# Three edits to a transformer layer on one core: the sample's attention in tiles of 128 rows, the selection masks inside the first gate projections, and another order of loads at the start of the second feed-forward product

## The chip, the cores and the metric

The kernel runs on one core of a Trainium2 chip. TensorE (PE) multiplies matrices, VectorE (DVE), ScalarE (ACT) and GpSimd (POOL) do the elementwise work, and SyncE (SP) issues most of the transfers between HBM and the core's memory. The metric is the device time of one execution in microseconds, less being better. Before is given as the median of three runs.

## What is computed

One layer is applied to a prompt of 1024 rows and to a sample of 64 rows that has 128 rows of cached keys and values. Both have 1024 channels. The reference, cut to what matters here:

```python
qa, ka, va, qi, ki, wi, qb, kb, vb, ga, gb = split(rmsnorm(x) @ w_in)     # 8 heads of 64 in each mixer
# mixer a: every query keeps the 256 visible keys with the best index score (sample: 48 of 192)
isc = sum_h wi[t, h] * relu(qi[t, h] . ki[s]);  keep = top_k(isc)
oa = softmax(qa . ka / 8 over keep) @ va
# mixer b: own chunk of 64 and the 8 chunks before it, with a bias by clipped distance
ob = softmax(qb . kb / 8 + bias) @ vb
x = x + (sigmoid(ga) * (oa @ w_o_a) + sigmoid(gb) * (ob @ w_o_b)) @ w_out
x = x + square(relu(rmsnorm(x) @ w_up)) @ w_down
```

The sample's queries see 192 keys in both mixers: the 128 cached ones and their own 64. The layer also returns the keys and values that it made.

## The kernel before

Every float32 operand is split into a high part (`hi`, an ACT copy into the matmul's reduced format) and a low part (`lo = raw - hi`, on DVE or POOL). Then three matmuls, hi by hi, hi by lo and lo by hi, make one product (`three`, lines 154 to 156). `two` (lines 162 and 163) does the same with a stationary operand that already holds both parts. `split` (line 143) makes a pair, with the low part on POOL unless `lo_on_vector` is set: line 146 is DVE's form and line 148 POOL's.

The program is written in an order of its own, and a planner then fixes the order of each engine and each queue. It goes by its own costs: an instruction goes out when the planner believes its operands to be ready, and among ready ones the earlier in the program goes first. `tc.issue_after(x)` keeps instructions behind `x` on the engine that `x` runs on. On the chip every engine and queue then works strictly in the planned order.

The stages, with their place in the profiled span:

- 0 to 155 us: norms, index keys and index scores. `stage_scores(i)` makes the scores of row block i (block 8 is the sample) in four PSUM banks called `s`. Into the last two blocks the first steps of `project_heads` are mixed (`between`). A step is the product of one row block with one 512-column weight: 24 matmuls, or 16 for the sample. It takes a bank called `acc` (two of them) or `wide` (four of them, on the space of `s`). The list `turn` says which: the first `FIRST` steps take `acc`, then one of every three does.
- 155 to 440 us: the other steps of `project_heads`, in the order vb, kb, qb, ka, va, qa. The weights come through two buffers `wraw` into eleven pairs `whi` and `wlo`. Beside this, `choose` finds for each row the score of its 256th best key, by 31 rounds of bisection on DVE and ACT, and then writes the masks of row blocks 2 to 7 (lines 571 to 584). `mask_s` is that of the sample.
- 440 to 490 us: the first four of 16 gate projections (`gate`), with their weights in the same `whi` and `wlo`.
- 490 to 800 us: attention, eight heads of mixer b and then eight of mixer a. The work on a head is in five groups: four pairs of row blocks, and the sample's 64 queries. `probs` makes scores (matmuls into `s`), adds bias or mask, and forms the softmax. `weigh` transposes the probabilities by PE, splits them, and multiplies by the values `vhl` into `po`. Eight more gate projections are laid between (`next_mark`). Their weights are in the pool `ring`. `ring` and attention's pool `at` are opened after the pools `tk` (the masks' temporaries), `pj`, `works` (the scores) and `fw` are closed, and take over their space.
- 800 to 1393 us: the other gates, the output projections, and the first feed-forward product.
- 1393 to 1738 us: the second feed-forward product, in four rounds of seven products P1, P2, P5, P6, P3, P7 and P4 (Strassen's scheme in Winograd's form). A product is 4 steps of 12 matmuls. The operands of the very first, `first_ops`, are made beforehand. All others are loaded from HBM (`left_source`, `right_source`) and split into slots of the pools `fx`, `fy` and `fz`. `few_operands` loads the sample's rows, and `few_rows` multiplies them. `take` adds the results up, and the last ones go out to `y_p`.

Of the kernel before, what the change touches and what calls it, by code (L numbers as in the profile page):

```python
# [18 lines left out]
P = 128  # L19
# [13 lines left out]
RING = 5  # L33
FIRST = 3
WARM = 18
# [9 lines left out]
def kernel(  # L45
# [97 lines left out]
    def split(raw, hi, lo, lo_on_vector=False):  # L143
        copy(hi, raw)
        if lo_on_vector:
            nc.vector.tensor_sub(lo, raw, hi)  # L146
        else:
            nc.gpsimd.tensor_sub(lo, raw, hi)  # L148
# [275 lines left out]
    def values_to_dram(t, rows, dst, r0):  # L424
        both = pj.tile([P, TP], F32R, tag="pair", name="pair", bufs=3).rearrange("p (h z d) -> p h z d", h=H, z=2)
        split(t[:rows].rearrange("p (h d) -> p h d", d=HD), both[:rows, :, 0], both[:rows, :, 1])
        nc.sync.dma_start(dst[r0:r0 + rows], both.bitcast(F32)[:rows])
# [54 lines left out]
    stage_scores(NT - 1, {3: heads, 7: heads})  # L482
    stage_scores(NT, {7: heads})
    close_pool("ix")

    masks = open_pool("masks")
    mask = {i: masks.tile([P, P * (i + 1)], BF16, name=f"mask{i}") for i in range(2, NT)}
    mask_s = masks.tile([TS, 192], BF16, name="mask_s")
    diag = masks.tile([P, 256], BF16, name="diag")
    nc.gpsimd.memset(diag, 0.0)  # L490
# [28 lines left out]
    def choose(vector, scalar):  # L519
# [50 lines left out]
        nc.vector.tensor_mul(thr, bits.bitcast(F32), sgn)  # L570
        for j, (i, w) in enumerate(zip(blocks, ws)):
            n = w.shape[1]
            over, same = (tk.tile([P, TP], BF16, tag="seen", name="seen", bufs=2) for _ in range(2))
            nth = tk.tile([P, TP], F32, tag="nth", name="nth", bufs=1)
            nc.vector.tensor_scalar(w, w, col(sgn, j), None, op0=ALU.mult)
            nc.vector.tensor_scalar(over[:, :n], w, col(thr, j), 0.0, op0=ALU.is_gt, op1=ALU.add, accum_out=col(cnt, j))
# [6 lines left out]
            nc.vector.tensor_add(over[:, :n], over[:, :n], same[:, :n])  # L583
            nc.gpsimd.tensor_scalar(mask[i], over[:, :n], -1.0, BIG, op0=ALU.add, op1=ALU.mult)

    def gate(m, ws, after=None):
# [9 lines left out]
    def load_head(mix, h, pool):  # L596
# [3 lines left out]
        for z in range(2):  # L600
# [6 lines left out]
                          v[:9 * P, h].rearrange("(t p) z d -> p t z d", p=P))  # L607
        nc.sync.dma_start(vhl[:TS, 9], v[9 * P:, h].rearrange("p z d -> p (z d)"))
        if mix == "b":
# [12 lines left out]
    with tc.issue_after(state["last"].ins):  # L622
        for _ in range(TOPK_S // 8):
            m8 = tk.tile([TS, 8], F32, tag="m8", name="m8", bufs=2)
            nc.vector.max(out=m8, in_=work_s)
            nc.vector.match_replace(out=work_s, in_to_replace=m8, in_values=work_s, imm_value=TAKEN)
        nc.vector.tensor_scalar(mask_s, work_s, 0.5 * (HIDDEN + TAKEN), -BIG, op0=ALU.is_gt, op1=ALU.mult)
        choose([2, 3, 4], [5, 6, 7])
    todo = [(mix, h) for mix in "ba" for h in range(H)]
    first_head = load_head(*todo[0], kv)  # L630
    for g in range(0, EARLY, 4):
        ws = []
        for k in range(KB):
# [4 lines left out]
            split(raw, hi, lo, lo_on_vector=True)  # L638
            ws.append((hi, lo))
        for q in range(4):  # L640
            gate(g + q, [(h[:, q * P:(q + 1) * P], l[:, q * P:(q + 1) * P]) for h, l in ws])
    for nm in ("tk", "pj", "works", "fw"):
        close_pool(nm)
# [15 lines left out]
    def attention(mix, h, t):  # L659
# [29 lines left out]
        def weigh(po, units):  # L689
            n = len(units)  # L690
            done = 0
            while done < n:
# [19 lines left out]
                for oo, (srcs, vt, krows, width, qo), idx in batch:  # L712
                    dst = po[:, qo:qo + width]
                    nc.tensor.matmul(dst, vhl[:krows, vt, :], ph[:krows, oo:oo + width], start=(idx == 0), stop=False)  # L714
                    nc.tensor.matmul(dst, vhl[:krows, vt, :], pl[:krows, oo:oo + width], start=False, stop=(idx == n - 1))  # L715

        def store(po, n, c0):
            half = at.tile([HD, 256], F32, tag="half", name="half", bufs=2)
            o = at.tile([HD, 256], F32, tag="o", name="o", bufs=3)
            copy(half[:, :n], po[HD:P, :n])  # L720
            nc.vector.tensor_add(o[:, :n], po[:HD, :n], half[:, :n])
            nc.sync.dma_start(o_dram[mix][cols, c0:c0 + n], o[:, :n])

        def soften(g):
            if g == 4:
                return [probs(TS, TP, TP, 192, bias[:, 384:576] if mix == "b" else mask_s)], None
            ms, first = [], []
# [13 lines left out]
        def mix_values(g, ms, first):  # L741
            po = bank("po", 256)
            if g == 4:
                weigh(po, [([(ms[0], 0, TS)], 8, P, TS, 0), ([(ms[0], P, TS)], 9, TS, TS, 0)])
                store(po, TS, TP)
                return
# [385 lines left out]
    dc = open_pool("dc", "right", reuse_waits="tile")  # L1132
    dp = open_pool("dp", reuse_waits="tile")
    fx = open_pool("fx", reuse_waits="tile")
    yp = open_pool("yp", reuse_waits="tile")
    slot = iter([place for place in ((fx, 8), (fy, 9), (fz, 6)) for _ in range(place[1])] * 20)

# [60 lines left out]
    QUAD = NPAIR // 4  # L1198
    q = {nm: [yp.tile([P, 512], F32, name=f"q_{nm}_{t}") for t in range(4)] for nm in ("P1", "P2", "P5", "P6", "P3", "P7", "P4")}
    y_few = yp.tile([TS, D], F32, name="y_few")  # L1200
    part = {"P2": (0, 0), "P3": (0, 512), "P4": (512, 0), "x": (512, 512)}
# [8 lines left out]
    def take(g, nm, t, ps):  # L1210
# [5 lines left out]
        if nm == "P7" and last:  # L1216
# [3 lines left out]
            return  # L1220
        if nm == "P4" and last:
            nc.vector.tensor_add(mine["P6"], ps, mine["P6"])
            nc.sync.dma_start(out_place(y_p, "P4", t), mine["P6"])
            return
        nc.vector.tensor_add(mine[nm], ps, mine[nm])
# [10 lines left out]
        elif nm == "P3":  # L1236
            nc.sync.dma_start(out_place(y_p, "P3", t), mine["P3"])

    for g in range(QUAD):
        few = few_operands(g)  # L1240
        for nm in ("P1", "P2", "P5", "P6", "P3", "P7", "P4"):
            at_end = nm == "P4" and g == QUAD - 1
            sums_here = [bank("x") for _ in range(4)]
            first = g == 0 and nm == "P1"
            if nm in ("P1", "P3"):
                few_sum = bank("few")
            ops = {}

            def few_rows(k):
                for z in range(2):  # L1250
# [4 lines left out]
            for k in range(4):  # L1255
# [3 lines left out]
                else:  # L1259
                    h = down_operand(left_source(nm, p), True)  # L1260
                    w = down_operand(right_source(nm, p), k < 3)
                ops[k] = h, w
                if at_end:
                    continue
                for t in range(4):
                    tok = slice(t * P, (t + 1) * P)
                    three(sums_here[t], [((h[0][:, tok], h[1][:, tok]), w)], k == 0, k == 3)
                if nm in KIND and not first:
                    few_rows(k)
            if first:  # L1270
                for k in range(4):
                    few_rows(k)
            if g == 0 and nm in part:
                for t in range(4):
                    nc.sync.dma_start(q[nm][t], out_place(x1_dram, nm, t))
                if nm == "P2":
                    nc.sync.dma_start(y_few, x1_dram[TP:])
            for t in range(4):
                if at_end:
                    tok = slice(t * P, (t + 1) * P)  # L1280
                    three(sums_here[t], [((ops[k][0][0][:, tok], ops[k][0][1][:, tok]), ops[k][1]) for k in range(4)])
                take(g, nm, t, sums_here[t])
            if nm in ("P2", "P7"):
# [8 lines left out]
            if nm == "P7" and g == QUAD - 1:  # L1292
                nc.sync.dma_start(y_s, y_few)
    for nm in ("dc", "fy", "fz", "yp", "fx", "dp"):
        close_pool(nm)
# [36 lines left out]
```

## Time and profile before

| | |
|---|---|
| median of three runs | 1738.48 us (1738.3 to 1742.39) |
| profiled execution, its own time | 1739.78 us |
| span of the profiled execution | 1738.0 us |
| mean granted TensorE clock | 0.997 |
| busy in the span: PE, DVE, ACT, POOL | 1709.3, 1199.3, 956.4, 481.4 us |
| bytes moved | 294.97 MB, 170 GB/s on the mean |

The span runs from the first to the last instruction of the profiled execution, and its own time is 1.8 us above its span. An engine's busy time counts its instructions and not the issue of transfers. The ends of matmuls are modelled, and neighbouring ones overlap in the records. So the pace of TensorE is read from start to start, and a stall from the idle time that the trace lists before an instruction.

### The profile page before, as it was taken

How to read it: one execution, taken by the hardware profiler on the slowest of the kernel's cores; microseconds unless marked ns; L12 is line 12 of the kernel's file. 1: busy time of each engine (PE TensorE's matmuls, PEld its weight loads, DVE VectorE, ACT ScalarE, POOL GpSimd, SP SyncE). 2: the span in 40 equal slices, each digit the busy share in tenths (PEclk: the TensorE clock that was granted, in tenths of full speed). 3: DMA queues.
4: the chain of work that ended last, by engine and by line, in shares of the span. 5: the costliest groups of instructions: out<-in, count | busy, mean ns of one | idle time of the engine just before them, and what ended most of it. 6: DMA issues, size and time to landing. Idle time of an engine off the chain costs nothing.

```text
span 1738.0 us, 30914 instructions
## 1 busy us (share of the span) xinstructions
PE 1709.3 (98%) x10540; PEld 1551.3 (89%) x10540; DVE 1199.3 (69%) x2765; ACT 956.4 (55%) x1994; POOL 481.4 (28%) x549
## 2 busy tenths in 40 slices
PE   8999999999999999999999999999999999999999
PEld 6877888877999999999999999999999978888887
DVE  6776799994447777774354345865587658868787
ACT  5785889722357777776443346644454447343430
POOL 2252432545424333332344354000000011111122
PEclk9999999999999999999999999999999999999999
DMA  5022475444667876664544559555566589565643
GB/s 175 8 81 104 149 201 151 152 161 161 180 162 191 198 176 153 159 146 134 170 137 136 185 163 284 168 184 183 186 209 204 165 300 316 183 199 149 199 124 103
DMA packets 277197, 294.97 MB, mean 170 GB/s; under 512 B 39792, under 2 KB 201584, under 8 KB 277040
## 3 DMA queue, kind: packets, MB, share of 16 engines
q1 hardware_dynamic: 248064, 257.61, 51.0%
q10 hardware_dynamic: 28976, 35.40, 5.8%
q8 instruction: 83, 1.36, 0.3%
q14 instruction: 74, 0.61, 0.1%
HBM read 199.85 MB, written 93.08 MB: 169 GB/s over the span
## 4 chain that ended last, share of the span: by engine, by line
PE 85%; DVE 6%; DMA 3%; issue 3%; ACT 2%; POOL 1%; SPq 0%; ACTq 0%; DVEq 0%; POOLq 0%
PE acc L154 9%; PE acc L156 9%; PE acc L155 9%; PE x L156 5%; PE x L155 5%; PE x L154 5%; PE pt L699 4%; PE wide L154 3%; PE wide L155 3%; PE wide L156 3%; PE s L162 3%; PE po L715 2%; PE s L163 2%; PE po L714 2%; PE pg L156 2%
## 5 line engine op out<-in xcount | busy, mean ns | idle before, releaser
L155 PE MATMUL x<-lo,hi 128*128 128x512 f32 x432 | 168.8, 391 | 2.3 <-POOL lo L148 1.7
L156 PE MATMUL x<-hi,lo 128*128 128x512 f32 x432 | 166.8, 391 | 0.0
L154 PE MATMUL x<-hi 128*128 128x512 f32 x432 | 164.2, 392 | 0.0
L148 POOL TENSOR_TENSOR lo<-wr,hi 128x512 fp32r<-128x512 f32 x15 | 35.1, 2343 | 455.6 <-ACT hi L123 455.6
L148 POOL TENSOR_TENSOR lo<-raw,hi 128x512 fp32r<-128x512 f32 x88 | 117.9, 1350 | 153.7 <-ACT hi L123 145.8
L123 ACT ACTIVATE hi<-raw 128x512 fp32r<-128x512 f32 x104 | 64.3, 627 | 90.4 <-PE acc L155 21.6
L711 DVE TENSOR_TENSOR pl<-pt,ph 128x512 fp32r<-128x512 f32 (+4 forms) x184 | 96.6, 545 | 19.5 <-ACT ph L123 18.9
L536 ACT ACTIVATE nth<-work,cand 128x768 bf16<-128x768 f32 (+2 forms) x93 | 96.6, 1039 | 18.3 <-DVE cand L553 14.1
L146 DVE TENSOR_TENSOR lo<-hr,hi 128x512 fp32r<-128x512 f32 x108 | 81.6, 756 | 28.9 <-ACT hi L123 28.7
L155 PEld LDWEIGHTS x<-lo,hi 128*128 128x128 f32 x432 | 81.1, 188 | 21.2 <-POOL lo L148 2.1
L123 ACT ACTIVATE ph<-pt 128x512 fp32r<-128x512 f32 (+4 forms) x184 | 81.6, 483 | 32.4 <-PE pt L699 25.6
L156 PEld LDWEIGHTS x<-hi,lo 128*128 128x128 f32 x432 | 81.1, 188 | 17.9
L154 PEld LDWEIGHTS x<-hi 128*128 128x128 f32 x432 | 81.1, 188 | 17.6
L154 PE MATMUL acc<-xnT,hi 128*128 128x384 f32 (+1 forms) x288 | 95.5, 331 | 0.0
L156 PE MATMUL acc<-xnT,lo 128*128 128x384 f32 (+1 forms) x288 | 94.3, 327 | 0.0
L155 PE MATMUL acc<-xnT,hi 128*128 128x384 f32 (+1 forms) x288 | 94.3, 327 | 0.0
L686 POOL TENSOR_SCALAR mw<-mw,sm 128x640 f32<-128x640 f32 (+1 forms) x64 | 56.7, 886 | 131.8 <-DVE sm L685 131.7
L154 PE MATMUL wide<-whi,xnT 128*128 128x512 f32 x224 | 89.4, 404 | 1.7 <-DVE work_s L366 1.7
L156 PE MATMUL wide<-whi,xnT 128*128 128x512 f32 x224 | 90.1, 402 | 0.0
L155 PE MATMUL wide<-wlo,xnT 128*128 128x512 f32 x224 | 89.9, 401 | 0.0
L714 PE MATMUL po<-ph,vhl 128*128 128x256 f32 (+2 forms) x336 | 86.0, 274 | 0.4 <-ACT ph L123 0.4
L715 PE MATMUL po<-pl,vhl 128*128 128x256 f32 (+2 forms) x336 | 85.9, 285 | 0.6 <-DVE pl L711 0.6
(671 smaller groups left out, 5963.2 us busy)
## 6 DMA issues: line engine op xcount, KB each, us to landing
hr<-h SPq DMA_DIRECT2D x108, 256.0 KB, 3.6
wr<-in_w_down_dram SPq DMA_DIRECT2D x76, 256.0 KB, 4.0
wraw<-in_w_in_dram SPq DMA_DIRECT2D x56, 256.0 KB, 2.8
h<-h ACTq DMA_DIRECT2D x32, 272.0 KB, 2.1
raw<-in_w_out_dram SPq DMA_DIRECT2D x32, 256.0 KB, 3.0
raw<-in_w_up_dram SPq DMA_DIRECT2D x32, 256.0 KB, 3.5
out_dram<-t SPq DMA_DIRECT2D x24, 256.0 KB, 2.4
g_dram<-gate SPq DMA_DIRECT2D x32, 192.0 KB, 3.2
```

Source lines behind the costliest of these rows:

```text
L123: return nc.scalar.activation(out, in_, AF.Copy)
L146: nc.vector.tensor_sub(lo, raw, hi)
L148: nc.gpsimd.tensor_sub(lo, raw, hi)
L154: nc.tensor.matmul(out, sh, mh, start=(opens and i == 0), stop=False, skip_group_check=resumes)
L155: nc.tensor.matmul(out, sh, ml, start=False, stop=False, skip_group_check=resumes)
L156: last = nc.tensor.matmul(out, sl, mh, start=False, stop=(closes and i == n - 1), skip_group_check=resumes)
L536: nc.scalar.activation(sign[:, :w.shape[1]], w, AF.Sign, bias=against, scale=-1.0, accum_out=col(cnt, j))
L686: nc.gpsimd.tensor_scalar(m[:rows, :n], m[:rows, :n], sm[:rows, 6:7], 1.0, op0=ALU.mult, op1=ALU.mult)
L699: nc.tensor.transpose(ps[:krows, oo:oo + qrows], m[:qrows, kc:kc + krows], ident[:qrows, :qrows])
L711: nc.vector.tensor_sub(pl[:kr, a:b], ps[:kr, a:b], ph[:kr, a:b])
L714: nc.tensor.matmul(dst, vhl[:krows, vt, :], ph[:krows, oo:oo + width], start=(idx == 0), stop=False)
L715: nc.tensor.matmul(dst, vhl[:krows, vt, :], pl[:krows, oo:oo + width], start=False, stop=(idx == n - 1))
```

## The change

- Scores: `FIRST` goes from 3 to 5, and the sample's `stage_scores` gets a projection step after its fourth head too. So four steps of `project_heads` stand ahead of the opening of `wide`, not three, and the first six take `acc`.
- Masks: `choose` ends with the threshold, and the scores get their sign back by an ACT copy with a scale (before: a DVE multiplication in the loop of masks). The loop's body becomes `mask_out`, which is called after the first gates and kept behind the last `lo` of their weights. `values_to_dram` makes the low part of mixer a's values on DVE, not on POOL.
- Sample's attention: `probs` runs on 128 query rows, the prompt's last 64 and the sample's 64. The sample's mask lies in the lower half of a tile `mask_below` (one transfer), and the bias is read 64 columns on. `weigh_sample` transposes two 128 by 128 tiles that overlap by 64 keys, and multiplies by full tiles of values, the second with zeros in its upper half.
- Second feed-forward product: the operands of P2 in round 0, the rows of the residual that it is added to, and the sample's residual are loaded ahead of the sample's rows. The sample's share of P1 is done inside P2. All low parts of round 0 are made on DVE. The slots go round in the order `fx`, `fz`, `fy`, and P2's sums get a pool of their own.
- The end: the last of the four result tiles is made and sent in two halves of 256 columns, the second by ACT's queue.

```diff
-FIRST = 3
+FIRST = 5
...
     def values_to_dram(t, rows, dst, r0):
-        split(t[:rows].rearrange("p (h d) -> p h d", d=HD), both[:rows, :, 0], both[:rows, :, 1])
+        split(t[:rows].rearrange("p (h d) -> p h d", d=HD), both[:rows, :, 0], both[:rows, :, 1],
+              lo_on_vector=dst is v_dram["a"])
...
-    stage_scores(NT, {7: heads})
+    stage_scores(NT, {3: heads, 7: heads})
...
-        for j, (i, w) in enumerate(zip(blocks, ws)):
+        for j, w in enumerate(ws):
+            nc.scalar.activation(w, w, AF.Copy, scale=col(sgn, j))
+
+        def mask_out(j):
+            i, w = blocks[j], ws[j]
...
-            nc.vector.tensor_scalar(w, w, col(sgn, j), None, op0=ALU.mult)
...
+        return mask_out
...
-        nc.sync.dma_start(vhl[:TS, 9], v[9 * P:, h].rearrange("p z d -> p (z d)"))
+        nc.gpsimd.memset(vhl[:TS, 9], 0.0)
+        nc.sync.dma_start(vhl[TS:, 9], v[9 * P:, h].rearrange("p z d -> p (z d)"))
...
-        choose([2, 3, 4], [5, 6, 7])
+        mask_out = choose([2, 3, 4], [5, 6, 7])
+    nc.sync.dma_start(mask_below[TS:], mask_s)
...
+        lows = last["lo"]
         for q in range(4):
             gate(g + q, [(h[:, q * P:(q + 1) * P], l[:, q * P:(q + 1) * P]) for h, l in ws])
+
+        with tc.issue_after(lows.ins):
+            for j in range(6):
+                mask_out(j)
...
+        def weigh_sample(po, m):
+
+            ps = ptile()
+            for j in range(2):
+                nc.tensor.transpose(ps[:, j * P:(j + 1) * P], m[:, j * TS:j * TS + P], ident)
+            v = ps[:, :2 * P].rearrange("p (j q) -> p j q", j=2)[:, :, TS:]
+            ph, pl = (at.tile([P, 512], F32R, tag=nm, name=nm, bufs=4) for nm in ("ph", "pl"))
+            halves = [t[:, :P].rearrange("p (j q) -> p j q", j=2) for t in (ph, pl)]
+            copy(halves[0], v)
+            nc.vector.tensor_sub(halves[1], v, halves[0])
+            for j in range(2):
+                nc.tensor.matmul(po[:, :TS], vhl[:, 8 + j, :], ph[:, j * TS:(j + 1) * TS], start=(j == 0), stop=False)
+                nc.tensor.matmul(po[:, :TS], vhl[:, 8 + j, :], pl[:, j * TS:(j + 1) * TS], start=False, stop=(j == 1))
...
-                return [probs(TS, TP, TP, 192, bias[:, 384:576] if mix == "b" else mask_s)], None
+                return [probs(P, TP - TS, TP, 192, bias[:, 448:640] if mix == "b" else mask_below)], None
...
-                weigh(po, [([(ms[0], 0, TS)], 8, P, TS, 0), ([(ms[0], P, TS)], 9, TS, TS, 0)])
+                weigh_sample(po, ms[0])
...
+    yr = open_pool("yr", reuse_waits="tile")
...
-    slot = iter([place for place in ((fx, 8), (fy, 9), (fz, 6)) for _ in range(place[1])] * 20)
+    slot = iter([place for place in ((fx, 8), (fz, 6), (fy, 9)) for _ in range(place[1])] * 20)
...
+    loaded = [(left_source("P2", k), right_source("P2", k)) for k in range(4)]
+    residual("P2")
+    nc.sync.dma_start(y_few, x1_dram[TP:])
+    late_rows = []
     for g in range(QUAD):
         few = few_operands(g)
...
-                    h = down_operand(left_source(nm, p), True)
-                    w = down_operand(right_source(nm, p), k < 3)
+                    src = loaded[k] if second else (left_source(nm, p), right_source(nm, p))
+                    h = down_operand(src[0], True)
+                    w = down_operand(src[1], k < 3 or g == 0)
...
+                if second and k == 0:
+                    for rows_of in late_rows:
+                        rows_of()
+                if first:
+                    late_rows.append(lambda k=k, rows=few_rows: rows(k))
+                elif nm in KIND:
                     few_rows(k)
-            if first:
-                for k in range(4):
-                    few_rows(k)
...
+                tok = slice(t * P, (t + 1) * P)
+                for z, queue in enumerate((nc.sync, nc.scalar)):
+                    c = slice(256 * z, 256 * (z + 1))
+                    if t == 3 or z == 0:
+                        wide = c if t == 3 else slice(0, 512)
+                        ps = bank("x") if t == 3 and z else sums_here[t]
+                        three(ps[:, wide], [((ops[k][0][0][:, tok], ops[k][0][1][:, tok]),
+                                                       [w[:, wide] for w in ops[k][1]]) for k in range(4)])
+                        nc.vector.tensor_add(q["P6"][t][:, wide], ps[:, wide], q["P6"][t][:, wide])
+                        queue.dma_start(out_place(y_p, "P4", t)[:, wide], q["P6"][t][:, wide])
```

## Rows read from the trace of the kernel before

**Rows 1.** The page's busy time of each engine.

```profile
PE 1709.3 (98%) x10540; PEld 1551.3 (89%) x10540; DVE 1199.3 (69%) x2765; ACT 956.4 (55%) x1994; POOL 481.4 (28%) x549
```

**Rows 2.** Stretches: length, busy PE, PEld, DVE, ACT, POOL, then clock, DMA, GB/s.

```profile
150.00:155.00 5.00, 2.66 (x18) 1.55 (x16) 3.42 (x9) 2.83 (x8) 0.14 (x1) 1.00 0.00 2
155.00:160.00 5.00, 4.86 (x14) 3.89 (x15) 5.00 (x17) 0.00 (x0) 0.69 (x4) 0.66 0.24 62
380.00:400.00 20.00, 14.46 (x58) 10.67 (x57) 17.97 (x13) 9.45 (x17) 14.55 (x10) 0.96 0.76 279
400.00:420.00 20.00, 20.00 (x84) 16.09 (x83) 7.69 (x24) 5.41 (x11) 10.54 (x11) 0.95 0.56 185
460.00:480.00 20.00, 20.00 (x125) 19.68 (x124) 0.69 (x2) 5.57 (x11) 6.33 (x5) 1.00 0.77 216
1400.00:1420.00 20.00, 20.00 (x89) 16.39 (x88) 9.17 (x14) 9.18 (x16) 1.28 (x1) 1.00 0.97 320
```

**Rows 3.** PE's waits: who was waited for, us in total, times, longest.

```profile
PE acc L154 <- ACT whi L123: 4.4, 2, 3.2
PE acc L155 <- POOL wlo L148: 1.1, 1, 1.1
...
PE x L155 <- POOL lo L148: 1.7, 1, 1.7
PE x L155 <- DVE lo L146: 0.6, 1, 0.6
```

**Rows 4.** DVE's timeline, masks and gates: start, length, instruction, idle before.

```profile
357.22 0.60 DVE L576 TENSOR_SCALAR_CACHE_REDUCE seen<-work,thr 128x384 bf16<-128x384 f32 x1
...
396.09 0.67 DVE L583 TENSOR_TENSOR seen<-seen 128x1024 bf16<-128x1024 bf16 x1
...
447.40 0.68 DVE L146 TENSOR_TENSOR wlo<-wraw,whi 128x512 fp32r<-128x512 f32 x1
```

**Rows 5.** PE's timeline: attention's first matmul, then one head's sample group.

```profile
490.52 0.22 PE L162 MATMUL s<-kh,qT 128*128 128x128 f32 x1
...
529.93 0.28 PE L714 MATMUL po<-ph,vhl 128*128 128x256 f32 x1
530.14 0.33 PE L699 MATMUL pt<-ident,m 64*128 64x64 f32 x2
530.40 0.39 PE L162 MATMUL s<-kh,qT 128*128 128x256 f32 x1
...
533.35 0.19 PE L715 MATMUL po<-pl,vhl 128*128 128x64 f32 x1
533.47 0.29 PE L714 MATMUL po<-ph,vhl 64*128 64x64 f32 x1
533.70 0.50 PE L162 MATMUL s<-kh,qT 128*128 128x512 f32 x1
534.03 0.40 PE L163 MATMUL s<-kl,qT 128*128 128x512 f32 x1
534.27 0.34 PE L154 MATMUL acc<-xnT,hi 128*128 128x384 f32 x1
...
534.62 0.34 PE L156 MATMUL acc<-xnT,lo 128*128 128x384 f32 x1
534.88 0.29 PE L715 MATMUL po<-pl,vhl 64*128 64x64 f32 x1
535.11 0.44 PE L699 MATMUL pt<-ident,mw 128*128 128x128 f32 x2
535.30 0.42 PE L162 MATMUL s<-kh,qT 128*128 128x384 f32 x1
```

**Rows 6.** ACT's and POOL's timelines, second feed-forward product, first round.

```profile
1415.72 0.64 ACT L123 ACTIVATE hi<-hr 128x512 fp32r<-128x512 f32 x1 [6.32 <-DMA hr<-h]
...
1426.14 5.19 POOL L148 TENSOR_TENSOR lo<-tc,hi 128x512 fp32r<-128x512 f32 x1 [15.37 <-ACT hi L123]
```

**Rows 7.** DVE's timeline: the last addition of the kernel.

```profile
1734.20 0.69 DVE L1222 TENSOR_TENSOR q_P<-x,q_P 128x512 f32<-128x512 f32 x1 [2.08 <-PE x L156]
```

More of the change, by code (lines that the diff above doesn't have):

```diff
@@ L145, in split @@
         if lo_on_vector:
-            nc.vector.tensor_sub(lo, raw, hi)
+            last["lo"] = nc.vector.tensor_sub(lo, raw, hi)
         else:
@@ L488 @@
     mask_s = masks.tile([TS, 192], BF16, name="mask_s")
+    mask_below = masks.tile([P, 192], BF16, name="mask_below")
+    nc.gpsimd.memset(mask_below[:TS], 0.0)
     diag = masks.tile([P, 256], BF16, name="diag")
@@ L1198 @@
     QUAD = NPAIR // 4
-    q = {nm: [yp.tile([P, 512], F32, name=f"q_{nm}_{t}") for t in range(4)] for nm in ("P1", "P2", "P5", "P6", "P3", "P7", "P4")}
-    y_few = yp.tile([TS, D], F32, name="y_few")
+    q = {nm: [(yr if nm == "P2" else yp).tile([P, 512], F32, name=f"q_{nm}_{t}") for t in range(4)]
+         for nm in ("P1", "P2", "P5", "P6", "P3", "P7", "P4")}
+    y_few = yr.tile([TS, D], F32, name="y_few")
     part = {"P2": (0, 0), "P3": (0, 512), "P4": (512, 0), "x": (512, 512)}
@@ L1220, in take @@
             return
[L1221 to L1224, printed above, removed]
         nc.vector.tensor_add(mine[nm], ps, mine[nm])
@@ L1237, in take, with residual @@
             nc.sync.dma_start(out_place(y_p, "P3", t), mine["P3"])
+    def residual(nm):
+        for t in range(4):
+            nc.sync.dma_start(q[nm][t], out_place(x1_dram, nm, t))
+    loaded = [(left_source("P2", k), right_source("P2", k)) for k in range(4)]
+    residual("P2")
+    nc.sync.dma_start(y_few, x1_dram[TP:])
+    late_rows = []
     for g in range(QUAD):
@@ L1243 @@
             sums_here = [bank("x") for _ in range(4)]
-            first = g == 0 and nm == "P1"
+            first, second = g == 0 and nm == "P1", g == 0 and nm == "P2"
             if nm in ("P1", "P3"):
@@ L1247, with few_rows @@
             ops = {}
-            def few_rows(k):
+            def few_rows(k, nm=nm, ops=ops):
                 for z in range(2):
@@ L1267 @@
                     three(sums_here[t], [((h[0][:, tok], h[1][:, tok]), w)], k == 0, k == 3)
-                if nm in KIND and not first:
-                    few_rows(k)
-            if first:
-                for k in range(4):
-                    few_rows(k)
[L1273 to L1277, printed above, removed]
-            for t in range(4):
[L1279 to L1282, printed above, removed]
+                if second and k == 0:
[4 more added lines that the diff above has]
+                elif nm in KIND:
+                    few_rows(k)
+            if g == 0 and nm in part and not second:
+                residual(nm)
+            for t in range(4):
+                if not at_end:
+                    take(g, nm, t, sums_here[t])
+                    continue
+                tok = slice(t * P, (t + 1) * P)
[8 more added lines that the diff above has]
+                        queue.dma_start(out_place(y_p, "P4", t)[:, wide], q["P6"][t][:, wide])
             if nm in ("P2", "P7"):
@@ L1293 @@
                 nc.sync.dma_start(y_s, y_few)
-    for nm in ("dc", "fy", "fz", "yp", "fx", "dp"):
+    for nm in ("dc", "fy", "fz", "yp", "fx", "yr", "dp"):
         close_pool(nm)
```

## The prediction

> **What bounds the kernel.** I read the page first. TensorE is busy for 98% of the span and no other engine for more than 69% [rows 1]. So an edit can pay in three ways: it ends a stall of PE, it keeps PE at its higher clock, or it takes time out of PE's own stream. Next I cut the span into stretches of 20 us, to see where PE is not busy or its granted clock falls. For most of the span it is busy 20 of 20 at 1.00. Of the exceptions, three lie where the diff acts: around 150 us, from 380 to 400 us, and shortly after 1420 us. Their stretches are in [rows 2]. The view of PE's waits names who was waited for in the last two [rows 3]. For the attention I read PE's timeline from start to start, since a busy share of 20 of 20 [rows 2] hides small gaps between neighbours of different shape [rows 5]. DVE's timeline shows the work that is moved, and where [rows 4].
>
> **Scores.** From 150 to 155 us PE is busy for 2.66 of 5 us [rows 2]. The sample's 16 short score matmuls stand alone there, each behind ACT's and DVE's work on the one before, and the first step in a `wide` bank has to wait for the `s` banks that they hold. Then the granted clock averages 0.66 from 155 to 160 us [rows 2]: between the levels 2.4 and 1.2 GHz, after the stretch in which PE stood idle for almost half. What can be had is 5.00 - 2.66 = 2.3 us of idle time and 5 x 0.34 = 1.7 us of clock, 4.0 us together. After the change six steps take `acc` at the start, of which the later ones need no `s` bank, so that a step of 24 matmuls can stand among the sample's. The planner places it by its own costs, and it may spend it earlier. Then nothing is gained, and that is the lower bound. I take 4.0, as before it has filled the gaps ahead of 150 us with just such steps. The mechanism that could eat it is a scores chain that ends later and delays `choose`. That is covered: only mixer a uses the masks, in the second half of attention, and they are now made behind the gates' weights.
>
> **Masks.** The stretch from 380 to 400 us shows 5.5 us of idle PE [rows 2]. The waits name the same sum: 4.4 for `whi` on ACT and 1.1 for `wlo` on POOL [rows 3]. These are the weights of the last projection. ACT itself is busy for only 9.45 of 20 us there, while DVE has 17.97 and POOL 14.55 [rows 2]. DVE is in the masks from 357.22 to 396.76 us [rows 4]. ACT's copies wait in their strict order for buffers that DVE's and POOL's late subtractions free. The clock then gives 0.96 and 0.95 in two stretches of 20 us, which is another 0.8 + 1.0 = 1.8 us [rows 2]. So 5.5 + 1.8 = 7.3 us hang on this place. The change takes the masks out of it. The ten low parts of mixer a's values come to DVE at 0.68 us each, by the same shape in [rows 4]: 7 us in place of 39.5. The six sign multiplications go to ACT, which has idle time there. If only POOL's and DVE's share goes and the chain of two weight buffers remains a limit, perhaps 3 us come back. I take 6.5 of 7.3.
>
> The masks go behind the last `lo` of the gates' weights. Before, that `lo` ends at 448.08 and attention begins at 490.52 [rows 4, 5], so there is room for 42.4 us, and DVE is busy for 0.69 of 20 us in the middle of it [rows 2]. The masks took 39.5 us in company of POOL and other DVE work. This cover is real but thin: 2.9 us. If PE comes earlier to this stage, the weights and the masks come earlier with it, and the room stays as it is. Queued behind the masks is what takes over the space of `tk` and `works`: the tiles of `at`, and `ring`'s weights for the gates inside attention. I cost it at nothing and keep it as a rival.
>
> **Sample's attention.** In [rows 5] a 512-column matmul next to its like takes 0.24 us (534.03 to 534.27), so 256 columns take 0.12 and 384 take 0.18. Around the 64-row forms it is different. The 256-column product ahead of the two small transposes takes 0.21 (0.09 more), the transposes take 0.26, and the two 64-row products take 0.23 each. The 512 columns behind the first of them take 0.33 (0.09 more), and the 384 columns ahead of the second take 0.26 (0.08 more). Two full transposes take 0.19 (535.11 to 535.30), and a full-height product of 64 columns 0.12 (533.35 to 533.47). So the 64-row parts cost 0.09 + 0.26 + 0.23 + 0.23 + 0.09 + 0.08 = 0.98 us a head. What replaces them costs 0.19 + 2 x 0.12 = 0.43, as two of the four products were there already. The difference is 0.55 us. The other heads repeat it to within some hundredths. The scores keep their 192 columns, and a wider stationary tile may add 0.03 for the pair (my estimate, a fraction of the 0.12). Sixteen heads give 16 x 0.52 = 8.3 us. Without the costs at entry and exit it would be (0.26 + 0.46 - 0.43 - 0.03) x 16 = 4.2, which is the lower bound. The upper is 8.8. ACT and DVE do one copy and one subtraction less per head, and POOL one small memset more. None of them is the limit here, as PE shows no idle time in this stage that the views list.
>
> The Trainium skill, "TensorEngine Tiling (Array Packing)", section "Tiling Modes", says that a change of the tiling mode, and not a mere change of tile, drains TensorE. The trace agrees with a cost of that kind: 0.08 to 0.09 us at three borders. The same page speaks against this change in "Performance Considerations": where the contracted dimension is 64 or less it advises row tiling, for up to twice the rate. By that, filling the tiles with zeros throws work away. What the 64-row form would then be worth here is the second rival below.
>
> **Second feed-forward product.** PE waits for 1.7 us for a `lo` on POOL and 0.6 for one on DVE [rows 3], 2.3 together. The POOL one took 5.19 us beside a busy DVE, and the cause lies further back: ACT had waited 6.32 us for a transfer [rows 6], in a stretch with the DMA engines at 0.97 [rows 2]. The change brings 2 MB of P2's operands ahead of the sample's rows. They are wanted when the DMA engines still have room, and P5's loads behind them come earlier on SP's queue. In this round the `lo` that took 5.19 is DVE's at 0.68. DVE gets six such more, 4 us over some 70 us. What is late next would be the sample's rows for P1, which now are loaded behind P2 and the residual. They are used only after P2's first 12 matmuls. I take 2.0, with 0 and 2.3 as bounds.
>
> **The end.** The last addition takes 0.69 us [rows 7], and from its end to the end of the span are 1738.0 - 1734.89 = 3.1 us of transfer. Half the columns take at best half of the addition, 0.35 us less. The transfer has half the bytes and a queue of its own: between 0 and 1.5 less, and I take 0.2, as its fixed part is unknown. Of the 24 half-width matmuls none was seen to cost more than its columns, so their price is nothing. That is 0.5, with 0.2 and 1.8 as bounds.
>
> **Sum.** 4.0 + 6.5 + 8.3 + 2.0 + 0.5 = 21.3 us. The profiled execution (1739.78, with a span of 1738.0) would come to 1718.5 and a span of 1716.7. The median of the runs is 1.3 us below that execution: 1738.48 - 21.3 = 1717.2, so 1717.
>
> **Rivals.**
>
> 1. Late masks hold up attention, and the kernel becomes slower. The place is the first tiles of `at` and `ring`. From a length of the mask chain of 42.4 us each microsecond more is one of idle PE, and the chain decides against the change from 42.4 + 21.3 = 64 us. For it speaks that the same chain took 39.5 us, stretched by POOL's work; POOL now has the last projection's work beside the first masks. Against it speaks the empty DVE in this stage. An overrun of 3 to 8 us gives 1720 to 1725. A loss needs the chain to grow by 60%.
> 2. The 64-row forms cost only their columns. If their price came from their place in the stream, and a 64-row product were worth the 0.12 of a full one, the gain per head would be 0.26 + 0.24 - 0.43 - 0.03 = 0.04, or 0.6 us in all. The time would be 1717.2 + 7.7 = 1725. Against it speak the same three borders with the same prices in all heads.
> 3. The starved stretches stay starved. The weights still pass through two buffers, and the transfers after 1400 us are as many as before. With 3 of 6.5 us and none of 2.0 the time is 1717.2 + 5.5 = 1723.
> 4. The change of `FIRST` does not do what it says: the planner spends the added steps before 150 us. That is 4.0 less, 1721.
>
> **How the numbers follow.** The forecast has 0.60, with a range of its own from 1713 to 1721. Late masks have 0.14, of which 0.03 end above the time before. Cheap 64-row forms have 0.08, starved stretches 0.11, and spent steps 0.07. All upper bounds together (4.0 + 7.3 + 8.8 + 2.3 + 1.8 = 24.2) give 1714. A new order by the planner may add as much again by chance in either direction as it has in small stalls here, some 3 us, so the low end is 1711. On the other side two rivals together give 1717.2 + 5.5 + 4.0 = 1727, so the high end is 1727. About 0.3% (5.2 us, a time of 1733.3 or 1743.7) is what a measurement of this kernel can tell from no change. Faster by more than that: all cases but the worst of the late masks and a few joint failures, 0.93. Within it: 0.03. Slower: 0.04.
>
> **What would show it.** Scores: PE busy near 5 of 5 from 150 to 155 us, and no stretch after it with a clock under 0.95. Masks: no wait for `whi` in the last projection, DVE's scans between the last `wlo` and attention's first matmul, and no idle PE at that matmul. Sample: no 64-row form in attention, and 0.5 us less per head from start to start. Second product: no wait of PE for `lo` in the first round. The end: under 3.5 us from the last matmul. The prediction is wrong if attention's first scores wait for DVE, or if PE's stream per head is as long as before.

## The result, and the profile after

The changed kernel takes 1721.41 us (median of four runs, 1716.99 to 1722.59), the kernel before 1739.95 in four runs: the three that gave 1738.48 and one more. The ratio is 0.9888 with a 95% interval of [0.9864, 0.9911]: 18.5 us less. The time lies inside the prediction's whole range (1711 to 1727) and 0.4 us above the range of the forecast itself (1713 to 1721). The profiled execution of after is the lowest of the four (1716.99, span 1715.2), so its trace shows 22.8 us. A second profile of the same kernel, from the experiments, is more typical: 1722.32, span 1720.4, where the median of its five runs is 1722.19. By the starts of the first or last matmul of each stage on PE's timeline, in us (the last row runs from the start of the last matmul):

| stage | before | after | after, second profile |
|---|---|---|---|
| start to attention's first matmul | 490.52 | 480.04 | 481.55 |
| to the first output projection | 361.14 | 351.33 | 351.22 |
| to the second feed-forward product | 541.71 | 540.81 | 541.77 |
| to its last matmul | 340.39 | 339.48 | 342.35 |
| to the end of the span | 4.24 | 3.54 | 3.51 |

The page of after, busy time of each engine (before: [rows 1]):

```profile
PE 1693.6 (99%) x10552; PEld 1548.0 (90%) x10552; DVE 1200.7 (70%) x2760; ACT 957.4 (56%) x1984; POOL 454.9 (27%) x550
```

Stretches of after, columns as in [rows 2]:

```profile
150.00:155.00 5.00, 5.00 (x27) 3.97 (x26) 1.50 (x4) 1.78 (x5) 0.48 (x2) 1.00 0.27 108
155.00:160.00 5.00, 5.00 (x27) 3.98 (x26) 1.97 (x5) 2.81 (x7) 1.29 (x1) 1.00 0.40 157
240.00:260.00 20.00, 18.57 (x88) 14.79 (x88) 18.02 (x65) 17.65 (x36) 2.70 (x3) 1.00 0.72 190
380.00:400.00 20.00, 20.00 (x87) 16.02 (x86) 9.68 (x27) 8.63 (x16) 2.59 (x2) 1.00 0.66 219
1460.00:1480.00 20.00, 18.84 (x83) 15.13 (x82) 17.34 (x28) 6.81 (x12) 4.21 (x3) 1.00 0.56 168
```

The holes at 150 us and from 380 to 400 us [rows 2] are closed, and the clock stays at 1.00. Two small holes are new, at 240 and at 1460 us. PE's waits of after name them: DVE's `pair` is the one at 240 us, DVE's `q_P` the one at 1460 us. The waits for `whi`, `wlo` and POOL's `lo` of [rows 3] are gone from their places. PE's timeline has two other new ones of over half a microsecond: 0.73 for an earlier weight's `whi` at 334.92, and 0.94 for POOL's `m` a few microseconds behind attention's first matmul (the last row here).

```profile
PE pt L411 <- DVE pair L417: 1.4, 1, 1.4
...
PE x L154 <- DVE q_P L1254: 1.2, 1, 1.2
```

```profile
484.31 0.33 PE L714 MATMUL pt<-ident,m 128*128 128x128 f32 x1 [0.94 <-POOL m L701]
```

DVE's timeline of after, the masks (before: [rows 4]): the last `wlo` of the gates, the first mask and the last one.

```profile
437.31 1.79 DVE L146 TENSOR_TENSOR wlo<-wraw,whi 128x512 fp32r<-128x512 f32 x1 [0.32 <-ACT whi L123]
439.02 0.60 DVE L582 TENSOR_SCALAR_CACHE_REDUCE seen<-work,thr 128x384 bf16<-128x384 f32 x1
...
470.49 0.69 DVE L589 TENSOR_TENSOR seen<-seen 128x1024 bf16<-128x1024 bf16 x1
```

The chain takes 32.2 us and ends 8.9 us ahead of attention. PE's timeline of after, attention's first matmul and one head's sample group (before: [rows 5]):

```profile
480.04 0.22 PE L162 MATMUL s<-kh,qT 128*128 128x128 f32 x1
...
519.68 0.28 PE L729 MATMUL po<-ph,vhl 128*128 128x256 f32 x1
519.80 0.38 PE L736 MATMUL pt<-ident,m 128*128 128x128 f32 x2
519.93 0.36 PE L162 MATMUL s<-kh,qT 128*128 128x256 f32 x1
...
521.83 0.25 PE L743 MATMUL po<-ph,vhl 128*128 128x64 f32 x1
521.91 0.42 PE L162 MATMUL s<-kh,qT 128*128 128x384 f32 x1
...
522.70 0.34 PE L156 MATMUL acc<-xnT,lo 128*128 128x384 f32 x1
522.88 0.19 PE L744 MATMUL po<-pl,vhl 128*128 128x64 f32 x1
522.91 0.27 PE L743 MATMUL po<-ph,vhl 128*128 128x64 f32 x1
523.01 0.28 PE L744 MATMUL po<-pl,vhl 128*128 128x64 f32 x1
523.13 0.48 PE L162 MATMUL s<-kh,qT 128*128 128x512 f32 x1
523.45 0.40 PE L163 MATMUL s<-kl,qT 128*128 128x512 f32 x1
```

From start to start the transposes take 0.13 and the four products 0.08, 0.03, 0.10 and 0.12, together 0.33. The 512 columns behind them still take 0.32. POOL's timeline of after, the low part ahead of PE's new wait (the slow one of before is a round earlier, [rows 6]):

```profile
1453.80 7.37 POOL L148 TENSOR_TENSOR lo<-wr,hi 128x512 fp32r<-128x512 f32 x1 [7.18 <-ACT hi L123]
```

DVE's timeline of after, the last addition (before: [rows 7]), now of half the columns:

```profile
1711.98 0.42 DVE L1329 TENSOR_TENSOR q_P<-x,q_P 128x256 f32<-128x256 f32 x1 [1.01 <-PE x L156]
```

### The profile page after: what moved, and what is told of

It reads as the page before. It is cut to its first block, busy times and chain, and to the rows that moved or that the text cites. A ratio compares the mean times of both kernels' runs of the same rounds, so it can differ in the third digit from the quotient of the medians.

```text
span 1715.2 us, 30888 instructions
## 1 busy us (share of the span) xinstructions
PE 1693.6 (99%) x10552; PEld 1548.0 (90%) x10552; DVE 1200.7 (70%) x2760; ACT 957.4 (56%) x1984; POOL 454.9 (27%) x550
## 5 line engine op out<-in xcount | busy, mean ns | idle before, releaser
L155 PE MATMUL x<-lo,hi 128*128 128x512 f32 (+1 forms) x436 | 169.2, 388 | 0.3 <-DVE lo L146 0.3
L156 PE MATMUL x<-hi,lo 128*128 128x512 f32 (+1 forms) x436 | 167.6, 389 | 0.0
L154 PE MATMUL x<-hi 128*128 128x512 f32 (+1 forms) x436 | 164.9, 390 | 1.2 <-DVE q_P L1254 1.2
L148 POOL TENSOR_TENSOR lo<-wr,hi 128x512 fp32r<-128x512 f32 x12 | 31.6, 2635 | 482.7 <-ACT hi L123 482.7
L155 PE MATMUL wide<-wlo,xnT 128*128 128x512 f32 x256 | 101.2, 398 | 0.0
L154 PE MATMUL wide<-whi,xnT 128*128 128x512 f32 x256 | 100.4, 398 | 0.7 <-ACT whi L123 0.7
L156 PE MATMUL wide<-whi,xnT 128*128 128x512 f32 x256 | 101.1, 397 | 0.0
L726 DVE TENSOR_TENSOR pl<-pt,ph 128x512 fp32r<-128x512 f32 (+2 forms) x152 | 90.9, 614 | 9.4 <-ACT ph L123 9.1
L123 ACT ACTIVATE ph<-pt 128x512 fp32r<-128x512 f32 (+3 forms) x168 | 79.7, 514 | 25.3 <-PE pt L714 16.3
L148 POOL TENSOR_TENSOR wlo<-wraw,whi 128x512 fp32r<-128x512 f32 x40 | 52.5, 1318 | 106.7 <-ACT whi L123 97.4
L123 ACT ACTIVATE hi<-wr 128x512 fp32r<-128x512 f32 x60 | 37.9, 631 | 75.5 <-issue 52.6
```

Of the source, the lines that this page charges most:

```text
L123: return nc.scalar.activation(out, in_, AF.Copy)
L154: nc.tensor.matmul(out, sh, mh, start=(opens and i == 0), stop=False, skip_group_check=resumes)
L155: nc.tensor.matmul(out, sh, ml, start=False, stop=False, skip_group_check=resumes)
L156: last = nc.tensor.matmul(out, sl, mh, start=False, stop=(closes and i == n - 1), skip_group_check=resumes)
L726: nc.vector.tensor_sub(pl[:kr, a:b], ps[:kr, a:b], ph[:kr, a:b])
```

## Experiments

**Each part alone.** Four kernels, each the kernel before with one part. Their edits are the lines of the diff above that belong to the part: scores (`FIRST`, `stage_scores`), masks, sample's attention, second product with the halves at the end.

> The kernel before with the scores' part alone: FIRST at 5 and a step of the projections after the sample's fourth head too. My theory (idle time and a low clock around 150 us end): 4.0 us less than before, PE busy all of 150 to 160 us at a clock of 1.00, attention's first matmul 4 us earlier. Rival (the planner spends the steps ahead of 150 us, or the step ends up as a stall elsewhere before attention): 0 to 1 us less, with a hole of the same size in another stretch between 140 and 490 us.

> The kernel before with the masks' part alone: the masks behind the gates' weights, the sign on ACT, the low parts of mixer a's values on DVE. My theory: 6.5 us less than before, no wait of PE for whi or wlo from 380 to 400 us, a clock of 1.00 there. Rival 1 (the two buffers of the weights remain a limit): 3 us less, and a wait for whi of 2 us or more remains. Rival 2 (late masks hold up attention): less than 3 us or a loss, with PE idle at attention's first matmuls behind POOL or DVE.

> The kernel before with the sample's attention in tiles of 128 rows alone. My theory (the 64-row forms cost at their borders too): 8.3 us less than before, or 9.8 by what the stage from attention's first matmul to the first output projection lost in the trace of the whole change. Rival (they cost only their columns): 0.6 us less, and the 9.8 of that stage came from the other edits, by a better order of its matmuls.

> The kernel before with the second feed-forward product's edits and the two halves at the end alone. My theory: 2.5 us less than before (2.0 by the operands and 0.5 by the end); by the trace of the whole change 1.6 (0.9 and 0.7), as the wait for a low part has gone only to the third product of the same round. Rival (the transfers are as many, so the starved stretch is only moved): 0.5 us less, all of it behind the last matmul.

Before took 1739.77 us there (23 runs).

| part alone | median | ratio and interval |
|---|---|---|
| scores | 1739.46 | 0.9998 [0.999, 1.0007] |
| masks | 1733.34 | 0.9961 [0.995, 0.9973] |
| sample's attention | 1729.03 | 0.9937 [0.9925, 0.9949] |
| second product and end | 1741.63 | 1.001 [1.0, 1.002] |

The scores alone gain nothing, although their own hole closes. The stretches of that kernel say where the 4 us went:

```profile
140.00:160.00 20.00, 20.00 (x96) 16.06 (x95) 8.45 (x14) 10.47 (x21) 3.99 (x4) 1.00 0.24 96
240.00:260.00 20.00, 18.22 (x79) 14.22 (x78) 18.84 (x63) 16.99 (x34) 4.28 (x4) 0.91 0.68 184
380.00:400.00 20.00, 13.93 (x50) 10.28 (x50) 19.29 (x18) 7.38 (x13) 12.65 (x10) 0.83 0.66 239
400.00:420.00 20.00, 18.80 (x81) 14.84 (x80) 18.90 (x35) 5.01 (x10) 8.87 (x8) 1.00 0.37 105
```

PE comes earlier to 240 us and waits there for DVE: 1.8 us idle and 20 x 0.09 = 1.8 of clock. Before, PE is busy there for 20 of 20 us at 1.00. And the scores end later, as they are now spread among other matmuls (the last one at 160.63, before at 153.22). The bisection hangs on them, and DVE's first mask stands at 369.08, 11.9 us later than before [rows 4]. Between 380 and 420 us PE loses 6.1 + 1.2 idle and 20 x 0.17 = 3.4 of clock, 10.7 us where before lost 7.3 [rows 2]. Of the idle time, 4.8 us are now waits for low parts on DVE. Attention begins at 491.98 in that profile; in three profiles with the code of before up to that point it begins at 490.52, 492.50 and 493.33. DVE's timeline and PE's waits of that kernel:

```profile
369.08 0.61 DVE L576 TENSOR_SCALAR_CACHE_REDUCE seen<-work,thr 128x384 bf16<-128x384 f32 x1
...
403.91 0.63 DVE L583 TENSOR_TENSOR seen<-seen 128x896 bf16<-128x896 bf16 x1
```

```profile
PE wide L155 <- DVE wlo L146: 4.8, 2, 3.6
```

The masks alone give 6.4 us, and their hole closes. Two small ones are new between 440 and 460 us (stretches of that kernel):

```profile
380.00:400.00 20.00, 20.00 (x87) 16.10 (x87) 8.34 (x10) 7.60 (x13) 3.70 (x3) 1.00 0.78 271
440.00:460.00 20.00, 18.10 (x113) 17.34 (x111) 18.43 (x38) 4.40 (x10) 11.85 (x17) 1.00 0.28 90
```

The sample's attention alone gives 10.7 us. The second product's part gives nothing or costs up to 3.5 us.

**The whole change without the second product.** Four kernels on one chip: without its loads and without the halves, the whole, with the halves alone, with the loads alone ("loads" stands for all edits of the second product but the halves).

> The whole change without its second feed-forward part and without the halves at the end. Alone, the scores gave 0.3 us, the masks 6.4, the sample's attention 10.7, and the second product with the end cost 1.9. Theory A (scores and masks pay together, as the 4 us that the scores save run into the masks' stall; the second product gives nothing): 10.5 by the start of attention in the trace of the whole change and 10.7 by the sample, 1739.8 - 21.2 = 1718.6, a little under the whole change. Theory B (the parts simply add, and the second product's edits give 2.5 in the whole): 1739.8 - 17.4 = 1722.4 or more, above the whole change by 2.

> The changed kernel once more, unaltered, for the comparison on one chip: 1721.4 by its first four times. If the profiled execution (1716.99) was a lucky one, the median stays within 1720 to 1722.6; if the others were disturbed, it comes nearer to 1717.

> The whole change without the second feed-forward part, but with the halves at the end. By the traces the end from the last matmul is 0.7 us shorter: 0.7 less than the whole change without both. Rival (24 shorter matmuls cost more than their columns): 0 or a loss.

> The whole change with the second feed-forward part, but without the halves at the end. If the loads are what cost time in most executions (theory A), 1 to 3 us above the whole change without both; by my forecast 2.0 below it.

Before took 1739.06 us.

| | without halves | with halves |
|---|---|---|
| without loads | 1717.62 (1716.79 to 1718.19) | 1718.47 (1715.96 to 1719.13) |
| with loads | 1720.55 (1718.92 to 1722.94) | 1722.19 (1721.64 to 1723.82) |

The loads cost 2.9 us without the halves and 3.7 with them. The kernel without both has a ratio of 0.9872 [0.9857, 0.9887] and is faster than the whole: theory A holds. The halves' 0.9 and 1.6 us lie inside the spreads, so they are not told from zero. In the traces the end behind the last matmul is 0.7 shorter with them (4.53 without both, 3.85 with the halves), and PE needs 0.2 longer for the last product (11.06 and 11.27 from the last `few` to the last matmul).

Where the loads cost is seen in the second profile of the whole change. POOL's, SyncE's (its waits, as in [rows 3]), DVE's and PE's views, and the stretch behind:

```profile
1447.60 1.31 POOL L148 TENSOR_TENSOR lo<-wr,hi 128x512 fp32r<-128x512 f32 x1 [373.50 <-ACT hi L123]
1456.12 8.75 POOL L148 TENSOR_TENSOR lo<-wr,hi 128x512 fp32r<-128x512 f32 x1 [7.21 <-ACT hi L123]
```

```profile
SPq L1190 <- POOL lo L148: 6.9, 1, 6.9
```

```profile
1473.32 0.69 DVE L1212 TENSOR_TENSOR wr<-wr,tc 128x512 f32<-128x512 f32 x1 [5.42 <-DMA wr<-in_w_down_dram]
```

```profile
1480.63 0.69 PE L154 MATMUL x<-hi 128*128 128x512 f32 x1 [2.29 <-DVE q_P L1254]
```

```profile
1480.00:1500.00 20.00, 19.37 (x77) 15.70 (x78) 16.79 (x26) 8.57 (x15) 2.58 (x2) 0.91 0.51 162
```

Read downward: POOL makes one low part of the second round while DVE works without a gap, and needs 8.75 us; the same shape took 1.31 just before, where DVE had a gap. That holds a `wr` buffer, so SyncE's queue waits 6.9 us before it can load into it. DVE waits 5.42 us for that load, its sums (`q_P`) come late, and PE waits 2.29 us for their bank. The clock behind it costs 20 x 0.09 = 1.8 us more.

While POOL's low part runs, DVE keeps its pace of 0.60 us from start to start. Two rows of that profile, and then the end of the same low part (at 1461.17) in the first profile:

```profile
1458.21 0.68 DVE L146 TENSOR_TENSOR lo<-hr,hi 128x512 fp32r<-128x512 f32 x1
1458.81 0.68 DVE L1199 TENSOR_TENSOR tc<-tc,wr 128x512 f32<-128x512 f32 x1
```

```profile
1459.51 0.68 DVE L1254 TENSOR_TENSOR q_P<-x,q_P 128x512 f32<-128x512 f32 x1
1460.11 1.61 DVE L1203 TENSOR_TENSOR tc<-wb,tc 128x512 f32<-128x512 f32 x1
```

**The price of 64 rows.** In the kernel without loads and halves, once the products and once the transposes go back to 64 rows. These two kernels and the next two ran on another chip than their bases; before took 1739.99 us there (7 runs), so the ratios to before stand beside the times.

```diff
-        nc.gpsimd.memset(vhl[:TS, 9], 0.0)
...
-                nc.tensor.matmul(po[:, :TS], vhl[:, 8 + j, :], ph[:, j * TS:(j + 1) * TS], start=(j == 0), stop=False)
-                nc.tensor.matmul(po[:, :TS], vhl[:, 8 + j, :], pl[:, j * TS:(j + 1) * TS], start=False, stop=(j == 1))
+                r = slice(j * TS, P)
+                nc.tensor.matmul(po[:, :TS], vhl[r, 8 + j, :], ph[r, j * TS:(j + 1) * TS], start=(j == 0), stop=False)
+                nc.tensor.matmul(po[:, :TS], vhl[r, 8 + j, :], pl[r, j * TS:(j + 1) * TS], start=False, stop=(j == 1))
```

> The whole change without its second feed-forward part and the halves (1717.6), in which the sample's second value product contracts only the lower 64 rows of the tile, in place of 128 with zeros above; the transposes stay whole. The result is the same. Theory (a 64-row form costs at its borders): 0.11 more for each of two products and 0.09 + 0.08 at the neighbours, 0.39 us a head, 6.2 us in all, 1723.8. Rival (it costs only its columns): within 0.6 us of 1717.6.

```diff
-                nc.tensor.transpose(ps[:, j * P:(j + 1) * P], m[:, j * TS:j * TS + P], ident)
+                nc.tensor.transpose(ps[:, j * TS:(j + 1) * TS], m[TS:, j * TS:j * TS + P], ident[TS:, TS:])
```

> The same base (1717.6), in which the sample's two transposes take only the lower 64 query rows, in place of 128 of which the upper half is thrown away; the products stay whole. Theory: 0.26 + 0.09 - 0.19 = 0.16 us a head, 2.6 us in all, 1720.2; with the products' 6.2 it makes 8.8, the upper bound of the forecast. Rival (half the rows are half the work): 0 to 1 us less than 1717.6.

They took 1722.47 (1721.09 to 1723.05) and 1721.37 (1721.21 to 1721.87), against 1717.62: 4.8 and 3.8 us more (by the ratios, 0.9899 and 0.9894 against 0.9872, it is 4.7 and 3.8; their intervals overlap a little). From attention's first matmul to the first output projection the traces have 354.58 and 354.72 where their base has 351.37, so 3.2 and 3.4 us lie in the stage itself. Half the rows cost more, not less. PE's timeline with 64-row products:

```profile
542.99 0.19 PE L744 MATMUL po<-pl,vhl 128*128 128x64 f32 x1
543.11 0.29 PE L743 MATMUL po<-ph,vhl 64*128 64x64 f32 x1
543.25 0.27 PE L744 MATMUL po<-pl,vhl 64*128 64x64 f32 x1
543.45 0.50 PE L162 MATMUL s<-kh,qT 128*128 128x512 f32 x1
543.78 0.40 PE L163 MATMUL s<-kl,qT 128*128 128x512 f32 x1
```

And with 64-row transposes:

```profile
538.63 0.27 PE L729 MATMUL po<-ph,vhl 128*128 128x256 f32 x1
538.84 0.34 PE L736 MATMUL pt<-ident,m 64*128 64x64 f32 x2
539.10 0.38 PE L730 MATMUL po<-pl,vhl 128*128 128x256 f32 x1
```

The first product takes 0.14, the second 0.20, and the 512 columns behind them 0.33. That last is no price of 64 rows: behind a full product of 64 columns they take 0.32 (523.13 to 523.45 in after), behind their like 0.24 [rows 5]. So the 3.2 us lie in the products themselves: from start to start, all products of 64 columns in the stage sum to 9.03 us there and to 5.71 in the base. The first costs less than the second, which has a full form behind it. Here the planner put the two side by side; before they stood apart [rows 5], each with a full form behind it at 0.23, which fits 3.2 in place of 6.2. The transposes take 0.26 in place of 0.13, and the 256 columns ahead of them 0.21 in place of 0.12.

**POOL's low part.** In the whole change the second round's low parts go to DVE; in the kernel without loads and halves only those of the first round do. The cut shows the one line of each that matters.

```diff
-                    w = down_operand(src[1], k < 3 or g == 0)
+                    w = down_operand(src[1], k < 3 or g <= 1)
```

> The whole change (1722.2 in the last call) with the low parts of the second product's second round on DVE too. In the changed kernel's second profile POOL's low part of P2's last weight takes 8.75 us beside a busy DVE, SyncE's queue waits 6.9 us for its buffer, the next weight lands late, and PE waits 2.3 us for a sum, with a clock of 0.91 in the stretch behind. Theory (POOL's low part is what costs): the wait and the drop go, 2.3 + 1.8 = 4.1 us less, 1718.1. Rival (DVE as a whole is late, and seven more low parts make it later): 1721 or more, with PE waiting for DVE in the first two rounds.

```diff
-                    w = down_operand(right_source(nm, p), k < 3)
+                    w = down_operand(right_source(nm, p), k < 3 or g == 0)
```

> The whole change without its second feed-forward part and the halves (1717.6), with one edit of that part put back: all low parts of the first round on DVE, no other order of loads. Theory (it is the order of the loads that moves the stall into the second round): the wait of 1.2 us for POOL's low part goes, 1716.4. Rival (with POOL out of the first round the next low part on POOL meets the same busy DVE, whatever the order of the loads): PE waits in the second round, 1718 to 1721.

The first took 1718.09 (1715.82 to 1718.86), 4.1 us under the whole change (by the ratios, 0.9873 against 0.99, it is 4.7; the intervals overlap). PE's waits and the stretch that had the hole:

```profile
PE x L155 <- DVE lo L146: 0.9, 1, 0.9
```

```profile
1460.00:1480.00 20.00, 20.00 (x89) 16.41 (x88) 18.26 (x32) 5.52 (x11) 0.00 (x0) 1.00 0.56 163
```

The second took 1718.58 (1716.08 to 1720.51): no gain, and the rival holds. With the old order of loads PE has the same new wait, behind the same low part on POOL (PE's and POOL's timelines):

```profile
1480.42 0.50 PE L154 MATMUL x<-hi 128*128 128x512 f32 x1 [2.06 <-DVE q_P L1256]
```

```profile
1457.10 6.50 POOL L148 TENSOR_TENSOR lo<-wr,hi 128x512 fp32r<-128x512 f32 x1 [6.44 <-ACT hi L123]
```

So it is not the order of the loads that moves the stall. Before, the same low part took 6.55 us as well, and PE did not wait for what followed.

```profile
1475.40 6.55 POOL L148 TENSOR_TENSOR lo<-wr,hi 128x512 fp32r<-128x512 f32 x1 [6.70 <-ACT hi L123]
```

PE does wait once DVE makes six low parts more and PE no longer stands still a round earlier; whether it needs both was not tried. By their medians the two kernels that avoid it, 1717.62 and 1718.09, are faster than both given ones, and not to be told from one another.

## Why the prediction held, and where it did not

**Scores and masks, 4.0 + 6.5.** Attention begins 10.5 us earlier in the first profile, as the sum said, and 9.0 in the second; that start itself differs by 2.8 between three profiles of before's code. But the terms are not independent, as the sum took them. The 4.0 is not there with the scores alone (0.3, inside its interval): PE arrives early at a stall that, by the rows, the late bisection makes longer. The prediction called a later scores chain covered, and that is so only because the masks are moved. The 6.5 for the masks came as 6.4 alone. Late masks as a rival did not occur: a chain of 32.2 us against room for 40.9 in after (439.10 to 480.04; the prediction had 42.4). The planner did not spend the scores' steps early.

**Sample's attention, 8.3.** It gave 10.7 alone and 9.8 in the whole, above the stated upper bound of 8.8. The difference of 0.9 is the wait for POOL's `m` and a smaller one behind it, 1.1 us in after and 0.2 before; the kernel with the masks alone has 1.0 of it, so it comes with the masks' part. That forms of 64 rows cost more than their columns was right, and the rival of cheap ones is excluded twice: 4.8 and 3.8 us more, where it allowed 0.6 or a gain.

Of the sum's terms two are off, in opposite directions. One is the third border, the 512 columns behind a 64-row product: they take 0.33 there and 0.32 behind a full one, so 0.08 of the 0.09 a head did not go. The other two borders stand, and both lie ahead of a 64-row form: 0.21 fell to 0.12 ahead of the transposes (519.68 to 519.80), and 0.26 to 0.18 for the 384 columns (522.70 to 522.88).

The other is the replacement, put at 0.43 a head. The transposes measured 0.13 for 0.19: the 0.19 was read behind a matmul of 64 columns (534.88), and in the sample's place 256 columns stand ahead. The four full products measured 0.33, so about 0.17 for two, for 0.24: the 0.12 was read right ahead of a 64-row form (533.47), and the same product now takes 0.03 (522.88 to 522.91). So 0.30 for 0.43, which makes 2.1 us in 16 heads, less the 1.3 of the third border. That gives 9.1; the rest up to 10.7 is not assigned to any term.

The Trainium skill, "TensorEngine Tiling (Array Packing)", "Performance Considerations", advises row tiling for 64 contracted rows. Both runs show a higher price for a few such forms one after another in a stream of full ones. Two of them at once, on the two halves of the rows, was not run.

**Second product, 2.0.** Here the sign was wrong: it cost 2.9 to 3.7 us. The step that failed is "In this round the `lo` that took 5.19 is DVE's at 0.68. DVE gets six such more", with the sample's rows named as what is late next. What was late next was the following low part on POOL, one round on, at 7.37 to 8.75 us. The prediction put nothing for a low part that still stays on POOL. Taking it away gave 4.1 us back; the 2.0 themselves never showed, since the kernel without this part is as fast as the mended one. Rival 3 thus held in its second half, "none of 2.0". The Trainium skill, "SBUF — State Buffer", "SBUF: two separate sides", describes a port pair that DVE with two inputs and GpSimd hold in turn for whole instructions, the other being blocked. The rows agree as far as POOL goes: 1.31 us and 8.75 for the same shape. They don't agree with a change of hands at every instruction: while POOL's low part ran, DVE kept its 0.60 (1458.21, 1458.81, 1459.41). DVE was held up once, when POOL's part ended: in the first profile its subtraction at 1460.11, right behind an addition that reads one operand from PSUM, took 1.61 us in place of 0.68. What lets POOL in was not tried.

**End, 0.5.** Net of PE's 0.2 the traces show 0.5. The times can't tell it from nothing.

**Sum.** 21.3 was forecast, 18.5 came by the medians. Without the second product's part it is 1739.06 - 1717.62 = 21.4. The number 1717 was too low by 4.4 for the kernel as changed. Some 1.5 of it is the start: before's median is 1739.95 with the fourth run, and 1738.48 without. The other 2.8 is the sum, and there luck helped: an excess of the sample's part of 1.5 to 2.4 hid a part of the error of 5 to 6 in the second product.

## What to carry to other kernels

Closing a stall early in a chain can be worth nothing until the next stall on the same chain is closed too, so time such edits together and alone. When work is moved away from an engine that is starved beside a busy neighbour, look for the next instruction of the same kind on it: the wait may go there. Among matmuls on all 128 rows, a few on 64 rows can cost more than full ones padded with zeros.

## What the runs showed that was not expected

The same stall can cost twice as much in one kernel as in another. From 240 to 260 us PE is busy for 18.22 of 20 us in the second profile of the whole change and in the kernel with the loads alone, whose programs are the same up to there. The granted clock is 0.91 in the first and 1.00 in the second, a difference of 1.8 us. The stretches of the two:

```profile
240.00:260.00 20.00, 18.22 (x82) 14.53 (x82) 18.18 (x61) 17.63 (x36) 3.63 (x3) 0.91 0.68 184
```

```profile
240.00:260.00 20.00, 18.22 (x87) 14.59 (x86) 18.02 (x64) 17.88 (x37) 2.96 (x3) 1.00 0.72 191
```

PE's one idle gap there is 1.78 us long in both. A mean of 0.91 says that PE ran for a part of the stretch at the lower of its two levels: from 246 to 248 us, 1.3 us behind the gap of the first, the first has 0.50 and the second 1.00. What decides whether it does was not tried. It may be a part of why the times of the whole change spread over 5.6 us (1716.99 to 1722.59 in its first four runs).
